# Two transformer blocks with a 32-expert MoE on one core: expert counts read into registers once, one extra path of 32 slots, bias load queued behind a weight tile

## The chip, the core and the metric

The kernel runs on one core of a Trainium2 chip. The metric is device time in microseconds (us) from the first to the last work of one execution. Before the change three runs took 1896.96, 1898.42 and 1899.1 us; their median, 1898.42 us, is the number that the change is measured against. The trace read here is a further execution of the same program, taken by the hardware profiler.

## The reference, cut to what matters

256 tokens of width 1024 pass a first block of two layers (attention, gated linear attention, dense feed-forward) and a second block whose feed-forward part is a mixture of 32 experts. Each token goes to its four best experts, and all arithmetic is in float32. The part that the change touches is the expert stage, with W = `w_gate_up` (32 x 1024 x 2048) and V = `w_down` (32 x 1024 x 1024):

```python
logits = (xt @ w_router) + b_router
top_v, top_i = lax.top_k(logits, 4)
gates = softmax(top_v)
for e in range(32):                       # as the reference's sorted blocks do it
    rows = tokens that chose e            # their number is the expert's count
    hdn = xt[rows] @ W[e] + b_gate_up[e]
    glu, lin = minimum(hdn[:, :1024], 7), clip(hdn[:, 1024:], -7, 7)
    y = (glu * sigmoid(1.702 * glu) * (lin + 1)) @ V[e] + b_down[e]
    out[rows] += gate[rows, e] * y
```

A count can be anything from 0 to 256, so the kernel must be right for all of them. The mean is 32 tokens per expert.

## The kernel before, in words

The program is unrolled: 32 copies of the expert's code follow one another. TensorE (PE) multiplies, VectorE (DVE) and ScalarE (ACT) evacuate and do the activation, GpSimd (POOL) makes small selectors, SyncE (SP) issues the weight loads. A scheduler places the instructions of each engine in an order close to that of the source, and every engine works its own list in that order.

**Weights.** An expert is 12 tiles of 1 MB, eight of W and four of V (`class Expert`, L1158). `etile` (L1149) hands out 18 buffers in the cyclic order of `RING2`, so 1.5 experts fit; the last of the 18 is the memory of `h`. SP issues one DMA for each tile (L1167 for W, L1175 for V), in order, and waits with each until the buffer's former readers are done. Ten tiles of expert 0 are issued while the second block's attention still runs (`EARLY`), the other two just before the expert loop (`first.rest()`).

**The 64 common slots.** `slots` (L1126) gives each token its place among an expert's tokens (`posm`) and writes the 32 counts and their maximum into `cnt`. `spread` (L1112) makes one-hot columns from it in `pos`, and `pick_up` (L1371) multiplies the tokens with them, so that `xt` holds the transposed inputs of two experts at a time: 64 slots of each of the two experts, and 64 further slots of each, 256 columns in all. `g1` (L1206) multiplies the 64 slots with W, `bias` (L1224) adds the bias through a one-hot selector `pick` that POOL writes, `act` (L1230) applies the activation, `g2` (L1242) multiplies with V, and `combine` (L1294) adds the result to the tokens.

**More than 64 tokens.** The count of an expert is needed in a register of PE, ACT and DVE, because each of the three branches on it. `count` (L1395) has POOL copy one number of `cnt` to a 1x1 tile (from expert 2 on behind POOL's last `pick`, by `issue_after`), and each of the three engines loads that number into a register. In the loop, `tc.If(n > 64)` (L1465) holds `extra_in` for slots 64 to 95 and, in a nested `tc.If(n > 96)` (L1467), a second `extra_in` for slots 96 to 127. After `g2` stands a second pair of branches (L1501, L1503) with `extra_out`. An engine whose branch isn't taken jumps over the code of the body. `extra_in` reads W and `extra_out` reads V, so that the buffers of W are given back behind the branch of L1465, those of V behind that of L1501.

**More than 128 tokens.** After the last expert, `many` (L1405) branches on the largest count, and would loop over all experts again, four chunks of 32 slots each.

**The expert biases.** `load_bias` (L1217) loads `b_gate_up` into `ball` on SP's queue, and ACT and DVE split it. It is traced in the loop's first turn, before `expert(1)` is loaded, and `bias(banks, 0)` needs it late in expert 0.

Of the kernel before, what the change touches and what calls it, by code (L numbers as in the profile page):

```python
# [9 lines left out]
F32 = mybir.dt.float32  # L10
BF16 = mybir.dt.bfloat16
F32R = mybir.dt.float32r
I32 = mybir.dt.int32
# [7 lines left out]
P = 128  # L21
T = 256
D = 1024
KC = D // P
DFF = 2816
NF = DFF // P
NE = 32
# [6 lines left out]
HOME = 99  # L34
RING2 = (-1, 0, 1, -1, 2, 3, 4, 5, 6, 7, -1, -1, 8, 9, 10, 11, 12, HOME)
EARLY = 10


C_ROPE = 0
# [56 lines left out]
def kernel_body(ctx, tc, I, out, stop=None, dbg=None):  # L96
    nc = tc.nc
# [10 lines left out]
    order = {}  # L108

    def nm(s):  # L110
        uid[0] += 1
        return f"{s}_{uid[0]}"
# [673 lines left out]
    with ExitStack() as cx:  # L786
# [44 lines left out]
        x = xT()  # L831
# [287 lines left out]
        def first_up(ts=(0, 1), kcs=range(KC)):  # L1119

# [37 lines left out]
        class Expert:  # L1158
# [4 lines left out]
            def load(self, n):  # L1163
                for _ in range(n):
                    r = etile()
                    if len(self.ws) < KC:
                        self.queue.dma_start(r, self.up(len(self.ws)))  # L1167
# [23 lines left out]
    with ExitStack() as cx:  # L1191
# [6 lines left out]
        now = mo.tile([P, 6, NE], F32, name="now", bufs=1)  # L1198
# [17 lines left out]

        def load_bias():  # L1217
            ball = mo.tile([P, 2, 512], F32, tag="yh", name="ball", bufs=1)
            for i in range(2):
                nc.sync.dma_start(ball[64 * i:64 * i + 64], I["b_gate_up"].rearrange("(b r) f -> r b f", b=2))  # L1220
            S.copy(bb, ball)
            V.tensor_sub(bb[64:], ball[64:], bb[64:].bitcast(F32))

# [146 lines left out]

        def pick_up(banks=None):  # L1371

            n = 2 if banks is None else 4
# [7 lines left out]
            x = mo.tile([P, KC, T], F32, tag="xt", name=nm("xt"), bufs=1)  # L1381
            for i, q in enumerate(banks):
                (V.tensor_copy if i % 2 else S.copy)(x[:, n * i:n * i + n, :512 // n], q.rearrange("p (a b) -> p a b", a=n))
            return x

        def begin(e, w):

            banks = [psum.tile([P, 512], F32, tag="g1", name=nm("g1")) for _ in range(2)]
            xe = xt[:, :, 64 * (e % 2):64 * (e % 2) + 64]
            g1(banks, xe, w.ws, range(AHEAD))  # L1390
            if e:
                bias(banks, e)
            return w, banks, xe, xt[:, :, P + 64 * (e % 2):P + 64 * (e % 2) + 64]

        def count(e):  # L1395

            ne = spool.tile([1, 1], I32, tag="ne", name=nm("ne"), bufs=2)
            if e > 1:
                with tc.issue_after(order[G].ins):
                    G.tensor_copy(ne, cnt[0:1, e:e + 1])  # L1400
            else:
                G.tensor_copy(ne, cnt[0:1, e:e + 1])
            return nc.values_load(ne[0:1, 0:1], engines=ARMS, min_val=0, max_val=T)

        def many(spare):  # L1405

            cmax = spool.tile([1, 1], I32, tag="ne", name="cmax", bufs=2)
            V.tensor_copy(cmax, cnt[0:1, NE:NE + 1])
            most = nc.values_load(cmax[0:1, 0:1], min_val=0, max_val=T)
            with tc.If(most > P):  # L1410
                V.tensor_scalar_add(now[:, 0:2, :], posm, -128.0)
                V.tensor_copy(now[:, 2:4, :], gate)
                V.tensor_copy(now[:, 4:6, :], qe)
                a1, pg = spare[:, :256], spare[:, 256:]
                with tc.For_i(0, NE, 1) as ei:
                    w = Expert(lambda kc: I["w_gate_up"][bass.ds(ei, 1), kc * P:(kc + 1) * P, :].rearrange("o p f -> (o p) f"),
                               lambda b: I["w_down_2"][bass.ds(ei, 1), b * 256:(b + 1) * 256, :].rearrange("o p f -> (o p) f"))
                    w.rest()
                    for c in range(4):
                        extra_in(a1, extra_xt(32 * c, lambda t: now[:, t, 0:1]), lambda q: now[:, 4 + q, 0:1], w.ws)  # L1420
                        extra_out(a1, 32 * c, lambda t: now[:, t, 0:1], lambda t: now[:, 2 + t, 0:1], w.wd, pg)
                    then = mo2.tile([P, T], F32, tag="oT", name="then", bufs=1)[:, :6 * NE].rearrange("p (a e) -> p a e", a=6)
                    V.tensor_copy(then[:, :, :NE - 1], now[:, :, 1:])
                    V.tensor_copy(now[:, :, :NE - 1], then[:, :, :NE - 1])
# [10 lines left out]
        n = count(0)  # L1435
        y = last = None
        for e in range(NE):
            j = e % 2
            w, banks, xe, xs = nxt
            if j == 0:  # L1440
                pT, gs = ahead
            if j and e + 1 < NE:
                spread(e + 1)
            if e == 0:
                load_bias()
                g1(banks, xe, w.ws, range(AHEAD, KC - 1))
                bias(banks, 0)
            g1(banks, xe, w.ws, range(KC - 1 if e == 0 else AHEAD, KC))
            through = order[TE].ins
            if e + 1 < NE:  # L1450
                nw = expert(e + 1)
# [10 lines left out]
            more = [mo2.tile([P, 256], F32, tag="og", name=nm("og"), bufs=2) for _ in range(2)]  # L1462
            pm, gt = (lambda t: posm[:, t, e:e + 1]), (lambda t: gate[:, t, e:e + 1])
            sel = lambda q: qe[:, q, e:e + 1]
            with tc.If(n > 64):  # L1465
                extra_in(more[0], xs[:, :, 0:32] if e > 1 else extra_xt(64, pm), sel, w.ws)
                with tc.If(n > 96):  # L1467
                    extra_in(more[1], xs[:, :, 32:64] if e > 1 else extra_xt(96, pm), sel, w.ws)
            if e + 1 == NE:
                gp2 = mo.tile([P, 2 * D], F32, tag="xt", name="gp2", bufs=1)  # L1470
# [6 lines left out]
            if e + 1 < NE:  # L1477
                after = count(e + 1)
            with tc.issue_after(through):
                if j and e + 1 < NE:  # L1480
                    xt = pick_up()
# [17 lines left out]
                    carry(fin)  # L1499
            g2(a, w.wd, y, j)  # L1500
            with tc.If(n > 64):  # L1501
                extra_out(more[0], 64, pm, gt, w.wd)
                with tc.If(n > 96):  # L1503
                    extra_out(more[1], 96, pm, gt, w.wd)
                if e + 1 == NE:
                    carry(fin, True)
            if e + 1 < NE:
                nxt = begin(e + 1, nw)
                n = after
            if j:  # L1510
                last = pT, y
        r = []
# [52 lines left out]
```

## Time and profile before

| what | us |
|---|---|
| runs: lowest, median, highest | 1896.96, 1898.42, 1899.1 |
| the profiled execution's own time | 1897.12 |
| its span, first to last instruction | 1895.3 |
| first matmul of expert 0 in the span (L1212) | 832.09 |
| PE busy in the span | 1715.2 |

The span is what the profile's rows add up to; 1.8 us lie around it, and the execution stands 1.3 us under the median. Some 832 us pass before the first matmul of the expert stage. In the rows below, PE is the matrix multiply, PEld the weight load that runs beside it, and an engine's name with q (PEq, SPq) its instruction sequencer. A float32 matmul leaves two records on PE and two on PEld. "Waited for" lists say what ended the idle time of an engine, with its sum and the number of times.

### The profile page before, as it was taken

What the parts mean: (1) busy time and instruction counts of PE and PEld (TensorE: products, weight loads), DVE (VectorE), ACT (ScalarE), POOL (GpSimd) and SP (SyncE); (2) the same over time, 40 slices, a digit from 0 to 9 for tenths busy, and PEclk for the clock granted to TensorE, in tenths of its full rate; (3) what the DMA queues carried; (4) which work ended last, traced back from release to release, by engine and by line L of the source; (5) the groups of instructions that cost most, each with busy time, mean ns of one, the idle gap of its engine ahead of it and who ended that gap; (6) DMA issues with size and microseconds to landing.
All of it is one profiled execution on the core that took longest, in us unless ns stands there. A gap on an engine that the chain in (4) does not pass through costs nothing. (4 is left out here: it accounts for less than half of the span.)

```text
span 1895.3 us, 23935 instructions
## 1 busy us (share of the span) xinstructions
PE 1715.2 (90%) x9400; PEld 1089.3 (57%) x9400; DVE 801.0 (42%) x1340; ACT 531.1 (28%) x906; POOL 161.6 (9%) x261
## 2 busy tenths in 40 slices
PE   7999999999999999998988888889898888888887
PEld 6887998788799879854333333324433333333332
DVE  5677776667777667542212121213222121212122
ACT  5645444564544446421011010101101110111011
POOL 1131220203122021000000000000000000000000
PEclk9999999999999999979999999999989999999999
DMA  9636788433588865559799999998889999999993
GB/s 307 160 123 203 242 280 298 135 134 123 192 264 273 287 210 181 201 232 372 304 400 409 390 383 412 402 401 339 330 334 414 416 385 397 392 414 401 405 398 117
DMA packets 161023, 571.27 MB, mean 301 GB/s; under 512 B 15490, under 2 KB 66188, under 8 KB 111636
## 3 DMA queue, kind: packets, MB, share of 16 engines
q1 hardware_dynamic: 149848, 553.47, 75.5%
q10 hardware_dynamic: 10140, 12.62, 2.0%
q0 software_dynamic: 800, 1.77, 0.8%
q8 instruction: 181, 2.97, 0.6%
q14 instruction: 54, 0.44, 0.1%
HBM read 564.11 MB, written 3.71 MB: 300 GB/s over the span
## 5 line engine op out<-in xcount | busy, mean ns | idle before, releaser
L1212 PE MATMUL g<-w,xt 128*64 128x512 f32 x2048 | 501.2, 606 | 100.3 <-PEq L1465 46.1
L1212 PEld LDWEIGHTS g<-w,xt 128*64 128x64 f32 x2048 | 157.7, 138 | 417.2 <-issue 411.6
L249 DVE TENSOR_TENSOR wlo<-w,whi 128x1024 fp32r<-128x1024 f32 x203 | 256.3, 1268 | 101.6 <-ACT whi L248 94.0
L248 ACT CAST whi<-w 128x1024 fp32r<-128x1024 f32 x203 | 211.2, 1046 | 176.4 <-PE ps L255 88.4
L1255 PE MATMUL ps<-w,aT 128*64 128x512 f32 x1024 | 230.2, 600 | 22.8 <-ACT aT L1249 22.8
L1233 DVE TENSOR_SCALAR g<-g 128x512 f32<-128x512 f32 x32 | 22.1, 692 | 490.5 <-PE g L1212 490.5
L254 PE MATMUL ps<-xh,whi 128*128 128x256 f32 x792 | 227.4, 287 | 0.0
L256 PE MATMUL ps<-xl,whi 128*128 128x256 f32 x792 | 223.4, 282 | 0.0
L255 PE MATMUL ps<-xh,wlo 128*128 128x256 f32 x792 | 223.3, 282 | 0.0
L1234 ACT ACTIVATE g<-g 128x512 f32<-128x512 f32 x32 | 19.3, 602 | 547.1 <-DVE g L1233 547.1
L1255 PEld LDWEIGHTS ps<-w,aT 128*64 128x64 f32 x1024 | 85.9, 138 | 145.8 <-issue 116.3
L254 PEld LDWEIGHTS ps<-xh,whi 128*128 128x128 f32 x792 | 149.4, 189 | 1.8 <-PE ps L403 1.2
L255 PEld LDWEIGHTS ps<-xh,wlo 128*128 128x128 f32 x792 | 149.2, 188 | 1.8 <-issue 1.4
L256 PEld LDWEIGHTS ps<-xl,whi 128*128 128x128 f32 x792 | 149.3, 188 | 0.0
L1258 DVE TENSOR_TENSOR yl<-ps,yh 64x512 fp32r<-64x512 f32 x64 | 44.1, 688 | 246.7 <-ACT yh L1257 245.7
L1257 ACT CAST yh<-ps 64x512 fp32r<-64x512 f32 x64 | 37.1, 579 | 230.2 <-PE ps L1255 229.4
L1226 POOL CAST pick<-qe 128x128 fp32r<-128x128 f32 x32 | 9.5, 296 | 970.5 <-PE g L1228 969.7
L254 PE MATMUL ps<-whi,xh 128*128 128x512 f32 x176 | 72.5, 412 | 2.0 <-ACT xh L212 1.1
L255 PE MATMUL ps<-whi,xl 128*128 128x512 f32 x176 | 71.0, 404 | 1.5 <-DVE xl L213 1.5
L256 PE MATMUL ps<-wlo,xh 128*128 128x512 f32 x176 | 70.4, 400 | 0.0
L489 DVE SCALAR_TENSOR_TENSOR modm<-w,cond,modm 128x512 f32<-128x512 f32 x84 | 65.4, 779 | 7.8 <-DMA w<-in_w_ada_dram 6.2
L746 POOL TENSOR_TENSOR al<-sg,ah 128x256 fp32r<-128x256 f32 x36 | 44.5, 1237 | 209.4 <-ACT ah L745 209.4
(375 smaller groups left out, 2343.4 us busy)
## 6 DMA issues: line engine op xcount, KB each, us to landing
w<-in_w_gate_up_dram SPq DMA_DIRECT2D x256, 1024.0 KB, 12.1
w<-in_w_down_dram SPq DMA_DIRECT2D x149, 1024.0 KB, 12.7
w<-in_w_in_dram SPq DMA_DIRECT2D x32, 1024.0 KB, 6.2
w<-in_w_ada_dram SPq DMA_DIRECT2D x24, 1024.0 KB, 5.2
w<-in_w_gate_dram SPq DMA_DIRECT2D x22, 1024.0 KB, 8.3
w<-in_w_up_dram SPq DMA_DIRECT2D x22, 1024.0 KB, 5.3
w<-in_w_out_dram SPq DMA_DIRECT2D x12, 1024.0 KB, 4.9
w<-in_w_in_dram SPq DMA_DIRECT2D x8, 512.0 KB, 8.8
```

Of the source, the lines that this page charges most:

```text
L248: S.copy(hv, self.raw)
L249: V.tensor_sub(lv, self.raw, hv.bitcast(F32))
L254: TE.matmul(o, lhsT=ah, rhs=bh, start=first, stop=False)
L255: TE.matmul(o, lhsT=al, rhs=bh, start=False, stop=False)
L256: order[TE] = TE.matmul(o, lhsT=ah, rhs=bl, start=False, stop=last)
L489: V.scalar_tensor_tensor(m, w, c, m, ALU.mult, ALU.add)
L746: G.tensor_tensor(out=al[:, f, :], in0=a, in1=ah[:, f, :].bitcast(F32), op=ALU.subtract)
L1212: order[TE] = TE.matmul(banks[b][64 * a:64 * a + 64, :], lhsT=xt[:, kc, :], rhs=ws[kc][:, c0:c0 + 512], start=kc == 0, stop=kc == KC - 1)
L1233: V.tensor_scalar(out=a, in0=gl, scalar1=7.0, scalar2=None, op0=ALU.min)
L1255: TE.matmul(q[at[b], :], lhsT=aT[:, f % 4, 64 * (f // 4):64 * (f // 4) + 64], rhs=wd[f // 2][:, c0:c0 + 512], start=f == 0, stop=f == KC - 1)
L1257: S.copy(y[0][at[b], b, :], q[at[b], :])
L1258: V.tensor_tensor(out=y[1][at[b], b, :], in0=q[at[b], :], in1=y[0][at[b], b, :].bitcast(F32), op=ALU.subtract)
```

## The change

It has four parts.

1. **Counts.** `count` is gone. Before the loop, one call loads all 32 numbers of `cnt` into registers of PE, ACT and DVE, checked against 0 and 256 as each number was before. POOL copies nothing, and `n = counts[e]` in the loop.
2. **Extra path.** Only slots 64 to 95 remain in the loop: one `extra_in` and one `extra_out` for each expert, no nested branch. `pos` shrinks from 256 to 192 columns, `pick_up` multiplies 192 instead of 256 columns and copies 384 instead of 512 columns of each bank, and the spare tile `og` has one buffer instead of two.
3. **Last branch.** `many` now runs from 97 tokens instead of 129. It loads each expert's count in its loop, skips experts that have no more than 96, and does five chunks from slot 96 on instead of four from slot 128 on.
4. **Bias load.** The first six tiles of expert 1 are issued before `load_bias`, and the two bias loads are ordered on SP behind the 18th tile.

The diff, cut:

```diff
-    pos = cpool.tile([P, 2, 2 * P], F32R, name="pos")
+    pos = cpool.tile([P, 2, 192], F32R, name="pos")
...
-                    for i in range(2 if e else 1):
-                        onehot(pos[:, t, P * i + 64 * j:P * i + 64 * j + 64], 64 * i, posm[:, t, e + j:e + j + 1])
+                    onehot(pos[:, t, 64 * j:64 * j + 64], 0, posm[:, t, e + j:e + j + 1])
+                    if e:
+                        onehot(pos[:, t, P + 32 * j:P + 32 * j + 32], 64, posm[:, t, e + j:e + j + 1])
...
+            with tc.issue_after(held):
+                for i in range(2):
+                    nc.sync.dma_start(ball[64 * i:64 * i + 64], I["b_gate_up"].rearrange("(b r) f -> r b f", b=2))
...
-                            TE.matmul(banks[kc // 2][:, T * (kc % 2):T * (kc % 2) + T], lhsT=part[:, t, kc * P:(kc + 1) * P], rhs=pos[:, t, :],
+                            TE.matmul(banks[kc // 2][:, 192 * (kc % 2):192 * (kc % 2) + 192], lhsT=part[:, t, kc * P:(kc + 1) * P], rhs=pos[:, t, :],
...
-        def count(e):
-
-            ne = spool.tile([1, 1], I32, tag="ne", name=nm("ne"), bufs=2)
-            if e > 1:
-                with tc.issue_after(order[G].ins):
-                    G.tensor_copy(ne, cnt[0:1, e:e + 1])
-            else:
-                G.tensor_copy(ne, cnt[0:1, e:e + 1])
-            return nc.values_load(ne[0:1, 0:1], engines=ARMS, min_val=0, max_val=T)
...
-            with tc.If(most > P):
-                V.tensor_scalar_add(now[:, 0:2, :], posm, -128.0)
+            with tc.If(most > 96):
+                V.tensor_scalar_add(now[:, 0:2, :], posm, -96.0)
...
+        counts = []
+        for i in range(0, NE, NREG):
+            counts += nc.values_load_multi_w_load_instructions(cnt[0:1, i:i + NREG], engines=ARMS, min_val=0, max_val=T)[1]
         xt = pick_up(g["xt"])
...
+            n = counts[e]
...
             if e == 0:
+                nw = expert(1)
+                nw.load(len(RING2) - KC - KC // 2)
+                held = order["load"].ins
                 load_bias()
...
             with tc.If(n > 64):
-                extra_in(more[0], xs[:, :, 0:32] if e > 1 else extra_xt(64, pm), sel, w.ws)
-                with tc.If(n > 96):
-                    extra_in(more[1], xs[:, :, 32:64] if e > 1 else extra_xt(96, pm), sel, w.ws)
+                extra_in(more, xs if e > 1 else extra_xt(64, pm), sel, w.ws)
...
             with tc.If(n > 64):
-                extra_out(more[0], 64, pm, gt, w.wd)
-                with tc.If(n > 96):
-                    extra_out(more[1], 96, pm, gt, w.wd)
+                extra_out(more, 64, pm, gt, w.wd)
```

`NREG` is 32, so the loop around the load runs once.

## Rows read from the trace of the kernel before

**Rows 1.** Windows: us, five engines' busy time, granted PE clock, DMA share, GB/s.

```profile
860.00:880.00 20.00, 19.50 (x214) 10.65 (x210) 2.16 (x5) 1.53 (x3) 0.00 (x0) 1.00 1.01 419
900.00:920.00 20.00, 18.38 (x134) 8.61 (x132) 4.63 (x12) 2.27 (x5) 0.00 (x0) 1.00 0.56 228
...
930.00:1272.00 342.00, 293.29 (x1338) 123.20 (x1340) 76.75 (x155) 36.90 (x74) 4.57 (x22) 0.99 0.98 399
1420.00:1831.00 411.00, 352.80 (x1642) 149.38 (x1640) 90.46 (x186) 46.07 (x94) 5.33 (x25) 1.00 0.99 403
```

**Rows 2.** Line L1212 (`g1`), whole span: PE's idle time, by what ended it, times.

```profile
  PEq L1465: 46.1, 28
  POOL ne L1400: 32.5, 25
  PEq L1501: 8.3, 7
  DMA w<-in_w_gate_up_dram: 6.9, 11
  PEq L1467: 5.2, 1
```

**Rows 3.** Line L1403 on PE's sequencer, whole span, then from 826 to 832 us.

```profile
L1403 PEldq TENSOR_LOAD <-ne x32: 302/308/487, 827.6 to 1795.1; - x32
L1403 PEldq FUSED_REGOPS  x32: 146/152/160, 828.1 to 1795.5; - x32
L1403 PEldq SEQ_ASSERT  x32: 18/18/26, 828.4 to 1795.7; - x32
...
L1403 PEldq TENSOR_LOAD <-ne x2: 312/400/487, 827.6 to 828.4; - x2
```

**Rows 4.** PE in order of time: around the first expert, and the last of `g1`.

```profile
827.48 3.78 PE L1123 MATMUL ps<-pos,xm 128*128 128x128 f32 x16 [0.71 <-DVE pos L1109]
832.09 5.53 PE L1212 MATMUL g<-w,xt 128*64 128x512 f32 x16 [0.83 <-issue]
...
1864.99 1.94 PE L1212 MATMUL g<-w,xt 128*64 128x512 f32 x8 [0.16 <-PEq L1465]
```

**Rows 5.** The branches on PE's sequencer: ns min/median/max; the fourth within 1300 to 1320 us.

```profile
L1465 PEldq COMPARE_BRANCH  x34: 70/6018/6452, 851.2 to 1860.4; - x34
...
L1501 PEldq COMPARE_BRANCH  x32: 70/3302/6760, 863.4 to 1878.7; - x32
...
L1467 PEldq COMPARE_BRANCH  x2: 556/3380/6203, 878.5 to 1315.4; - x2
...
L1467 PEldq COMPARE_BRANCH  x1: 556/556/556, 1315.4 to 1315.4; - x1
...
L1503 PEldq COMPARE_BRANCH  x4: 187/261/348, 915.4 to 1341.5; - x4
```

**Rows 6.** PE's records in the branches' bodies, each by its line.

```profile
L1334 PE MATMUL ps<-w,xt x128: 376/379/403, 1310.2 to 1317.7; 128*32 128x256 f32 x128
...
L1328 PE MATMUL ps<-bb,qe x32: 379/379/403, 872.0 to 1310.0; 128*32 128x256 f32 x32
...
L1319 PE MATMUL ps<-opos,xmh x16: 254/263/263, 868.3 to 871.7; 128*128 128x32 f32 x16
...
L1367 PE MATMUL ps<-w,oaT x128: 378/379/403, 909.0 to 1337.5; 128*32 128x256 f32 x128
...
L1342 PE MATMUL ps<-oaT,oT x32: 374/446/479, 913.1 to 1340.9; 32*128 32x256 f32 x32
```

**Rows 7.** Line L1379 (`pick_up`): half of its matmuls, the other half alike.

```profile
L1379 PE MATMUL ps<-pos,xmh x240: 273/280/582, 893.1 to 1812.5; 128*128 128x256 f32 x120
```

**Rows 8.** SP's queue in order of time, 796 to 858 us.

```profile
796.71 3.66 SPq L1175 DMA_DIRECT2D w<-in_w_down_dram  x3
828.10 1.39 SPq L1220 DMA_DIRECT2D ball<-in_b_gate_up_dram  x2
829.53 27.81 SPq L1167 DMA_DIRECT2D w<-in_w_gate_up_dram  x8
```

More of the change, by code (lines that the diff above doesn't have):

```diff
@@ L36 @@
 EARLY = 10
+NREG = 32
 C_ROPE = 0
@@ L1166, in load @@
                     if len(self.ws) < KC:
-                        self.queue.dma_start(r, self.up(len(self.ws)))
+                        order["load"] = self.queue.dma_start(r, self.up(len(self.ws)))
                         self.ws.append(r)
@@ L1197, in kernel_body @@
         bb = mo.tile([P, 2, 512], F32R, name="bb", bufs=1)
-        now = mo.tile([P, 6, NE], F32, name="now", bufs=1)
+        now = mo.tile([P, 9, NE], F32, name="now", bufs=1)
         qe = mo.tile([P, 2, NE], F32, name="qe", bufs=1)
@@ L1218, in load_bias @@
             ball = mo.tile([P, 2, 512], F32, tag="yh", name="ball", bufs=1)
-            for i in range(2):
-                nc.sync.dma_start(ball[64 * i:64 * i + 64], I["b_gate_up"].rearrange("(b r) f -> r b f", b=2))
+            with tc.issue_after(held):
+                for i in range(2):
+                    nc.sync.dma_start(ball[64 * i:64 * i + 64], I["b_gate_up"].rearrange("(b r) f -> r b f", b=2))
             S.copy(bb, ball)
@@ L1371, in pick_up @@
         def pick_up(banks=None):
-            n = 2 if banks is None else 4
+            n, c = (2, 192) if banks is None else (4, P)
             if banks is None:
@@ L1378, in pick_up @@
                         for i, part in enumerate((xmh, xml)):
-                            TE.matmul(banks[kc // 2][:, T * (kc % 2):T * (kc % 2) + T], lhsT=part[:, t, kc * P:(kc + 1) * P], rhs=pos[:, t, :],
+                            TE.matmul(banks[kc // 2][:, 192 * (kc % 2):192 * (kc % 2) + 192], lhsT=part[:, t, kc * P:(kc + 1) * P], rhs=pos[:, t, :],
                                       start=kc % 2 + t + i == 0, stop=kc % 2 + t + i == 3)
-            x = mo.tile([P, KC, T], F32, tag="xt", name=nm("xt"), bufs=1)
+            x = mo.tile([P, KC, 192], F32, tag="xt", name=nm("xt"), bufs=1)
             for i, q in enumerate(banks):
-                (V.tensor_copy if i % 2 else S.copy)(x[:, n * i:n * i + n, :512 // n], q.rearrange("p (a b) -> p a b", a=n))
+                (V.tensor_copy if i % 2 else S.copy)(x[:, n * i:n * i + n, :c], q[:, :n * c].rearrange("p (a b) -> p a b", a=n))
             return x
@@ L1392, in begin @@
                 bias(banks, e)
-            return w, banks, xe, xt[:, :, P + 64 * (e % 2):P + 64 * (e % 2) + 64]
-        def count(e):
-            ne = spool.tile([1, 1], I32, tag="ne", name=nm("ne"), bufs=2)
-            if e > 1:
-                with tc.issue_after(order[G].ins):
-                    G.tensor_copy(ne, cnt[0:1, e:e + 1])
-            else:
-                G.tensor_copy(ne, cnt[0:1, e:e + 1])
-            return nc.values_load(ne[0:1, 0:1], engines=ARMS, min_val=0, max_val=T)
+            return w, banks, xe, xt[:, :, P + 32 * (e % 2):P + 32 * (e % 2) + 32]
         def many(spare):
@@ L1409, in many @@
             most = nc.values_load(cmax[0:1, 0:1], min_val=0, max_val=T)
-            with tc.If(most > P):
-                V.tensor_scalar_add(now[:, 0:2, :], posm, -128.0)
+            with tc.If(most > 96):
+                V.tensor_scalar_add(now[:, 0:2, :], posm, -96.0)
                 V.tensor_copy(now[:, 2:4, :], gate)
                 V.tensor_copy(now[:, 4:6, :], qe)
+                V.tensor_copy(now[:, 6, :], cnt[:, :NE])
+                V.tensor_scalar_add(now[:, 7:9, :], posm, -224.0)
@@ L1414, in many @@
                 a1, pg = spare[:, :256], spare[:, 256:]
                 with tc.For_i(0, NE, 1) as ei:
[L1416 to L1421, printed above, removed]
@@ L1422, in many @@
-                    then = mo2.tile([P, T], F32, tag="oT", name="then", bufs=1)[:, :6 * NE].rearrange("p (a e) -> p a e", a=6)
-                    V.tensor_copy(then[:, :, :NE - 1], now[:, :, 1:])
-                    V.tensor_copy(now[:, :, :NE - 1], then[:, :, :NE - 1])
+                    one = spool.tile([1, 1], I32, tag="ne", name="one", bufs=2)
+                    V.tensor_copy(one, now[0:1, 6, 0:1])
+                    with tc.If(nc.values_load(one[0:1, 0:1], min_val=0, max_val=T) > 96):
+                        w = Expert(lambda kc: I["w_gate_up"][bass.ds(ei, 1), kc * P:(kc + 1) * P, :].rearrange("o p f -> (o p) f"),
+                                   lambda b: I["w_down_2"][bass.ds(ei, 1), b * 256:(b + 1) * 256, :].rearrange("o p f -> (o p) f"))
+                        w.rest()
+                        for c in range(5):
+                            pm = lambda t: now[:, 7 * (c // 4) + t, 0:1]
+                            extra_in(a1, extra_xt(32 * (c % 4), pm), lambda q: now[:, 4 + q, 0:1], w.ws)
+                            extra_out(a1, 32 * (c % 4), pm, lambda t: now[:, 2 + t, 0:1], w.wd, pg)
@@ L1426, in many @@
+                    for i in range(0, 9, 3):
+                        then = mo2.tile([P, T], F32, tag="oT", name="then", bufs=1)[:, :3 * NE].rearrange("p (a e) -> p a e", a=3)
+                        V.tensor_copy(then[:, :, :NE - 1], now[:, i:i + 3, 1:])
+                        V.tensor_copy(now[:, i:i + 3, :NE - 1], then[:, :, :NE - 1])
             turn[0] -= KC + KC // 2
+        counts = []
+        for i in range(0, NE, NREG):
+            counts += nc.values_load_multi_w_load_instructions(cnt[0:1, i:i + NREG], engines=ARMS, min_val=0, max_val=T)[1]
@@ L1434, in kernel_body @@
             ahead = places(), slot_gates(0)
-        n = count(0)
         y = last = None
@@ L1450, in kernel_body @@
             if e + 1 < NE:
-                nw = expert(e + 1)
+                nw = expert(e + 1) if e else nw
                 nw.rest()
@@ L1461, in kernel_body @@
                 G.memset(acc, 0.0)
-            more = [mo2.tile([P, 256], F32, tag="og", name=nm("og"), bufs=2) for _ in range(2)]
+            more = mo2.tile([P, 256], F32, tag="og", name=nm("og"), bufs=1)
             pm, gt = (lambda t: posm[:, t, e:e + 1]), (lambda t: gate[:, t, e:e + 1])
@@ L1465, in kernel_body @@
             with tc.If(n > 64):
-                extra_in(more[0], xs[:, :, 0:32] if e > 1 else extra_xt(64, pm), sel, w.ws)
-                with tc.If(n > 96):
-                    extra_in(more[1], xs[:, :, 32:64] if e > 1 else extra_xt(96, pm), sel, w.ws)
+                extra_in(more, xs if e > 1 else extra_xt(64, pm), sel, w.ws)
             if e + 1 == NE:
-                gp2 = mo.tile([P, 2 * D], F32, tag="xt", name="gp2", bufs=1)
+                gp2 = mo.tile([P, KC * 192], F32, tag="xt", name="gp2", bufs=1)
                 gp2, spare = gp2[:, :D], gp2[:, D:D + 512]
@@ L1476, in kernel_body @@
                 many(spare)
-            if e + 1 < NE:
-                after = count(e + 1)
             with tc.issue_after(through):
@@ L1508, in kernel_body @@
                 nxt = begin(e + 1, nw)
-                n = after
             if j:
```

## The prediction, made before the changed kernel was run

> **What bounds the kernel now.** I read the windows first [rows 1]. Over the steady stretches of the expert loop (930 to 1272 and 1420 to 1831 us) the DMA engines show a share of 0.98 and 0.99 at 399 and 403 GB/s, and PE is busy 86%. Both look nearly full, so the question is who waits for whom. The window 860 to 880 us, with loads queued throughout, reaches 419 GB/s, so the transfers still have holes of 4 to 5%. The list of what ended PE's idle time before `g1` [rows 2] settles it: 46.1 us went to the branch of L1465 on PE's own sequencer (28 times, 1.65 us each), 32.5 us to POOL's copy of the count (25 times, 1.30 us), 8.3 us to the branch of L1501, and only 6.9 us to weights that hadn't landed. PE sets the pace, and the buffers that it gives back late are the holes in the transfers. The floor behind it is near: a tile is 128 x 2048 float32, 1.049 MB, so an expert's 12 tiles take 12.58 MB / 419 GB/s = 30.0 us, against 12.58 / 0.401 = 31.4 us at the present mean rate.
>
> **The counts.** What goes is POOL's copy behind each `pick` and the three loads behind it: 32.5 us of PE's idle time [rows 2]. The remaining `pick` of POOL has no other customer and stays hidden. What comes is 32 values at once on PE, ACT and DVE, just ahead of expert 0. On PE a value costs a load of 0.308 us and a check of 0.152 us, plus an assertion that takes 0.018 us, 0.48 us in all [rows 3]; 32 of them are 15.3 us. They start about 827.6 us [rows 3] while PE still works through L1123, and expert 0 starts at 832.09 anyway [rows 4], which hides 4.5 us. That leaves **+11 us** in front of expert 0, where everything on PE queues behind it. The bounds: one load for all 32 with 32 checks, 0.31 + 32 x 0.17 = 5.8 us, or +1; and 0.8 us for a value, as the two at 827.6 and 828.4 stand apart [rows 3], 26 us, or +21. I take 0.48 because it is the median of 32 cases. ACT and DVE have no check and are done earlier. [...]
>
> **The branches.** A branch that isn't taken jumps over its body, and on PE that takes very different times [rows 5]. I measure a body in PE records, each with a weight load beside it [rows 6]: `extra_in` has 128 (L1334) + 16 (L1328, 32 in two) = 144, so 288 instructions; `extra_out` has 64 (L1367) + 16 (L1342) and a few transposes, about 168. Today L1465 skips two `extra_in`, 576 instructions, at a median of 6.0 us; L1501 skips 336, at a median of 3.3 us and up to 6.76, and only 7 of its 32 passes cost PE time [rows 2]; the nested L1467 skips 288 at expert 14 and took 0.556 us, while at expert 1, where the body also has 32 matmuls of `extra_xt`, 352 took 6.2 us; the nested L1503 skips 168 and never took over 0.348 us [rows 5]. PE's queue holds matmuls for 6.0 - 1.65 = 4.4 us meanwhile, so that only jumps near 6 us cost PE time. The change makes L1465 a jump of 288 and L1501 one of 168. By the rows, 168 is always short. For 288 there is one case, short; at 336 between a fifth and a quarter are long. I let 1 in 7 stay long, 4 of 28: 4 x 1.65 = 6.6 us stay of the 46.1, **-39.5 us**, and **-8.3 us** at L1501. Bounds: all short, -46; all as now, 0. The nested jump at L1467 goes with its **-5.2 us** [rows 2]. In the two experts that do have more than 64 tokens, no nested body ran, so that no count is over 96: `many` still skips, and its new loop costs nothing.
>
> **The narrower `pick_up`.** 15 calls of 32 matmuls. One takes 0.280 us at 256 columns [rows 7] and 0.263 us at 32 [rows 6], so 64 columns fewer are worth 64/224 x 17 ns = 5 ns: 480 x 5 ns = **-2 us**. The copies of 384 instead of 512 columns on ACT and DVE, and the shorter one-hot writes on DVE, run beside `g2` and cost or give nothing; PE doesn't wait for them now.
>
> **The bias load.** In the queue of SP the last tile of expert 0 is issued by 800.4 us, then the bias load holds the queue until 828.10, and expert 1's first tiles follow from 829.53 [rows 8]. The change lets six tiles, 6 x 2.5 = 15 us of transfer, go into that gap. I cost it at **0**: after those six the 18 buffers are full in either order, and the next can't start before expert 0 gives its W back at its branch, which starts at 851.2 us [rows 5]. PE doesn't wait for these tiles before. If the six come free only after 820 us, the bias lands up to 15 us later than now, about 847 us, which is when expert 0 wants it; with the 11 us of register loads in front it still isn't late.
>
> **The sum.** PE: -32.5 - 39.5 - 8.3 - 5.2 - 2 + 11 = -76.5, a span of 1895.3 - 76.5 = 1819 us. The transfers allow: first release at 851.2 + 11 = 862 us, 366 tiles left x 1.049 MB / 419 GB/s = 916 us, and the hole at expert 1's `extra_out` (228 of 419 GB/s in 900 to 920 us, 9 us [rows 1]) stays: the last tile lands at 1787. The last tile of W lands four tiles, 10 us, ahead of it, at 1777; from the last of `g1` (1864.99) to the end PE needs 1895.3 - 1865.0 = 30.3 us [rows 4]: 1807 us. With two limits this close, each now and then waits for the other. Of today's holes (4.3% of 900 us, 39 us) I let 15 us stay. Span 1819 + 15 = 1834, and with the 1.8 us around the span the execution takes 1836; the profiled execution lies 1.3 us under the median, which I let go into the rounding: **1836 us**.
>
> **Rivals.**
> - *The long jump stays.* L1465 takes 6 us at 288 instructions too. For it: one short case at 288 against one long at 352, and a jump in three staying long would already take 9 us more than I allow. Then PE gains -32.5 - 5.2 - 2 - 8.3 + 11 = -37: 1858, and with some 5 us of transfer waits 1865 us. [...]
> - *The transfers are at their limit already.* The share of 0.98 to 0.99 is the true ceiling and 419 GB/s holds for 20 us only. Then the loop gains 1 to 2% of 930 us, 14 us, and expert 1's nested jump 5, against +11 in front: 1890 us. Against it speak 6.9 us of PE waits for weights in the whole loop.
> - *Slower.* The register loads sit in front of expert 0 at the high price (0.8 us for a value, +21 us), and the transfers are at their limit as above, with the loop gaining its 1% (9 us) and expert 1's jump 5: +21 - 14 = +7, so 1904 us. It decides from +18 on, 0.70 us for a value, and only where the loop can't give time back.
> - *Nothing happens where it counts:* the scheduler leaves the branches behind another late signal of the same length (the next `pick` of POOL in place of the copy), and the gains at the jumps pay for the loads: within 4 us of now.
>
> **How the numbers follow.** The forecast gets 0.60, with 1812 to 1856 as its own range: loads from +1 to +21, jumps from -46 to -33, stayed holes from 0 to 30 us, not all at one end. The long jump gets 0.20 (1855 to 1878), transfers at their limit 0.10, slower 0.05, nothing 0.05. The range of 1810 to 1872 takes in the forecast and most of the long jump. A measurement tells 0.2%, about 4 us, from no change. Faster by more: 0.60 + 0.20 + most of 0.10 and a little of the rest, 0.90; same 0.05; slower 0.05.
>
> **What would show it.** No POOL copy of counts and no PE wait for it; PE's branch of L1465 mostly under 4 us and its wait list near 7 us instead of 46; expert 0 starting near 843 us; the windows of the loop at 410 to 418 GB/s, and PE waiting for weights for tens of us instead of 6.9; six tile issues ahead of the bias load in SP's queue. The prediction is wrong if the jumps stay at 6 us, if the loads take far from 15 us, or if the rate stays at 400 GB/s while PE waits for weights.

## The result, and the profile after

The changed kernel takes 1830.57 us (median of four runs, 1825.96 to 1833.62) where the kernel before took 1897.69 us in the same session: a ratio of 0.9649, with a 95% interval of 0.963 to 0.9668. The profiled execution took 1830.35 us, with a span of 1828.2. Line numbers have moved: the branch behind `g1` is L1472 (L1465 before), the one behind `g2` L1504 (L1501), `g1` itself L1215 (L1212), the register load L1431 and the branch of `many` L1404.

First the windows of the expert loop, columns as in [rows 1]:

```profile
868.50:900.00 31.50, 30.85 (x282) 17.89 (x284) 9.06 (x25) 5.71 (x13) 0.00 (x0) 1.00 0.97 397
900.00:960.00 60.00, 55.26 (x290) 21.20 (x286) 11.49 (x24) 4.63 (x9) 0.59 (x2) 0.97 0.98 403
960.00:1260.00 300.00, 281.76 (x1330) 114.21 (x1328) 74.10 (x162) 36.76 (x78) 2.95 (x10) 0.99 1.01 418
1260.00:1400.00 140.00, 126.52 (x738) 53.18 (x736) 35.07 (x80) 15.29 (x33) 1.71 (x6) 0.95 0.97 401
1400.00:1780.00 380.00, 355.74 (x1635) 139.66 (x1633) 88.64 (x178) 43.77 (x90) 3.84 (x13) 1.00 1.01 418
1780.00:1796.00 16.00, 12.59 (x54) 3.52 (x52) 0.00 (x0) 0.00 (x0) 0.00 (x0) 1.00 0.87 359
```

In the steady stretches (960 to 1260 and 1400 to 1780 us) PE is busy 94% instead of 86%, and the transfers run at 418 GB/s instead of 399 to 403. The holes that PE used to leave in them are gone, except around the two experts with extra tokens (868.5 to 960 us, and 1260 to 1400) and in the last tiles. Next, what PE waited for from 860 to 1830 us (its own waits alone: sum in us, times, longest), the first two lines those of the kernel before and the rest those of the changed one:

```profile
PE g L1212 <- PEq L1465: 44.1, 26, 2.2
PE g L1212 <- POOL ne L1400: 32.5, 25, 1.5
```

```profile
PE ps L1259 <- ACT aT L1253: 22.0, 30, 0.7
PE g L1215 <- PEq L1472: 15.8, 27, 4.2
PE ps L1251 <- DVE g L1244: 8.6, 14, 0.8
PE ps L1346 <- DMA yl<-in_b_down_dram: 4.2, 1, 4.2
PE fin L1312 <- PEq L1404: 4.1, 1, 4.1
PE g L1215 <- SPq L1404: 3.4, 4, 1.9
PE g L1215 <- DMA w<-in_w_gate_up_dram: 2.0, 4, 0.6
```

The wait for POOL's copy is gone. The wait for the first branch fell from 44.1 to 15.8 us, and the second branch no longer appears. The short waits for `aT` were there before (21.3 us) and stayed. The branches themselves, on PE's sequencer (count: shortest/median/longest in ns, first and last start), beside [rows 5], and the register loads beside [rows 3]:

```profile
L1472 PEldq COMPARE_BRANCH  x34: 70/335/6215, 863.2 to 1792.9; - x34
L1472 PEldq EVENT_SEMAPHORE  x30: 51/51/51, 868.5 to 1794.8; - x30
...
L1504 PEldq COMPARE_BRANCH  x34: 70/330/2705, 877.4 to 1811.7; - x34
...
L1431 PEldq FUSED_REGOPS  x32: 146/146/160, 831.6 to 840.5; - x32
L1431 PEldq SEQ_ASSERT  x32: 18/18/24, 831.9 to 840.7; - x32
L1431 PEldq TENSOR_LOAD <-cnt x1: 2333/2333/2333, 829.2 to 829.2; - x1
```

The median jump at the first branch is 0.335 us where it was 6.018. Listed one by one, 5 of the 30 that are jumped (experts 2, 11, 12, 17 and 27) still take about 6 us. All 32 values come with a single load of 2.33 us, but the 32 checks behind it run from 831.6 to 840.7 us, 0.28 us each. The second line is used below: it is the point behind a jumped branch at which PE gives the tiles of W back. Its first time, 868.5 us, is the first release of W, its last belongs to the last expert; before, it ran from 856.5 to 1864.9 us. Last, SP and PE by time, at the start of the loop and at its end (start, us, what, and in brackets the idle time before it), beside [rows 4] and [rows 8]:

```profile
814.78 14.04 SPq L1170 DMA_DIRECT2D w<-in_w_gate_up_dram  x6
828.87 1.39 SPq L1224 DMA_DIRECT2D ball<-in_b_gate_up_dram  x2
868.62 0.82 SPq L1170 DMA_DIRECT2D w<-in_w_gate_up_dram  x2
...
829.12 3.78 PE L1126 MATMUL ps<-pos,xm 128*128 128x128 f32 x16 [0.70 <-DVE pos L1111]
840.86 4.57 PE L1215 MATMUL g<-w,xt 128*64 128x512 f32 x12 [7.96 <-issue]
...
1792.85 1.94 PE L1215 MATMUL g<-w,xt 128*64 128x512 f32 x8 [1.88 <-SPq L1404]
1795.34 1.94 PE L1215 MATMUL g<-w,xt 128*64 128x512 f32 x8 [0.55 <-SPq L1404]
1801.35 6.49 PE L1312 MATMUL fin<-acc,idio 128*128 128x512 f32 x8 [4.08 <-PEq L1404]
```

Six tiles stand ahead of the bias load, and then SP issues nothing until the first release. At the end PE takes the last tiles of W one at a time, 2.49 us apart, which is 1.049 MB / 418 GB/s = 2.51 us: there it follows the transfers.

### The profile page after: what moved, and what is told of

Read it like the earlier page. It is cut to its first block, busy times and chain, and to the rows that moved or that the text cites. A ratio compares the mean times of both kernels' runs of the same rounds, so it can differ in the third digit from the quotient of the medians.

```text
span 1828.2 us, 23744 instructions
## 1 busy us (share of the span) xinstructions
PE 1710.2 (94%) x9400; PEld 1068.3 (58%) x9400; DVE 795.9 (44%) x1340; ACT 528.2 (29%) x906; POOL 157.4 (9%) x229
## 5 line engine op out<-in xcount | busy, mean ns | idle before, releaser
L1215 PE MATMUL g<-w,xt 128*64 128x512 f32 x2048 | 502.6, 604 | 33.9 <-PEq L1472 15.8
L1215 PEld LDWEIGHTS g<-w,xt 128*64 128x64 f32 x2048 | 153.6, 138 | 354.6 <-issue 328.0
L1259 PEld LDWEIGHTS ps<-w,aT 128*64 128x64 f32 x1024 | 71.9, 138 | 157.5 <-issue 126.1
L1262 DVE TENSOR_TENSOR yl<-ps,yh 64x512 fp32r<-64x512 f32 x64 | 44.1, 689 | 251.3 <-ACT yh L1261 250.3
```

The costliest lines, as they stand in the source:

```text
L1215: order[TE] = TE.matmul(banks[b][64 * a:64 * a + 64, :], lhsT=xt[:, kc, :], rhs=ws[kc][:, c0:c0 + 512], start=kc == 0, stop=kc == KC - 1)
L1259: TE.matmul(q[at[b], :], lhsT=aT[:, f % 4, 64 * (f // 4):64 * (f // 4) + 64], rhs=wd[f // 2][:, c0:c0 + 512], start=f == 0, stop=f == KC - 1)
L1262: V.tensor_tensor(out=y[1][at[b], b, :], in0=q[at[b], :], in1=y[0][at[b], b, :].bitcast(F32), op=ALU.subtract)
```

## The experiments

The kernel before ran beside each: its median was 1895.26 us beside the first four told here, 1894.68 beside "the whole body twice" and "fewer bytes", and 1897.68 beside the rest. Since these medians differ by 3 us, a small difference from the changed kernel is also given by the ratios, each to the kernel before that ran beside it. They stand here by what they ask.

**Part 1 alone.** The kernel before with all counts loaded at once:

```diff
-            if e + 1 < NE:
-                after = count(e + 1)
+            n = counts[e]
```

> The kernel before with the first part alone: all counts loaded at once, the nested branch, the 256 columns and the bias load as before. Theory (PE set the pace before, the transfers set it after the whole change): PE loses the 32.5 us of waits for the counts and gains 7 to 11 us of loads in front of expert 0; the jumps at the first branch stay near 6 us with some 40 us of idle time, so PE still sets the pace: 1868 to 1878 us. Rival (the count and the jump are one wait, and without the count the jump hides itself behind a fuller queue): the jumps' idle time falls too, under 1855 us. Rival (the loads cost more than the waits): 1890 us or more.

Measured 1889.28 us, ratio 0.997 (0.9954 to 0.9986): 6 us of gain where 17 to 27 were expected. PE's waits from 860 to 1830 us in this kernel:

```profile
PE g L1214 <- PEq L1470: 48.7, 28, 2.0
...
PE g L1214 <- PEq L1504: 8.8, 9, 1.1
PE ps L1381 <- issue: 8.5, 5, 3.3
...
PE g L1214 <- issue: 3.9, 1, 3.9
```

The 32.5 us of waits for POOL's copy are gone, but the branch costs 4.6 us more than before and the two "issue" waits, which came to 1.9 us before, 12.4. Between the first and the last release the loop took 993.7 us (862.5 to 1856.2) against 1008.4: 14.7 us won. The first release came 6.0 us later, and the stretch behind the last release grew from 30.4 to 34.6 us. That makes -14.7 + 6.0 + 4.2 = -4.5 us, the difference of the two spans (1890.8 and 1895.3). This wait did not take its whole length with it (14.7 of 32.5 us): about half of it covered sequencer time that then showed by itself. These "issue" waits stand behind long jumps (the one of 3.9 us begins at 1122.2 us, 0.8 us after a jump of 6.2 us); what they are, no row names.

**Parts 2 to 4 alone.** The changed kernel with a copy and three loads per expert again:

```diff
-            n = counts[e]
+            if e + 1 < NE:
+                after = count(e + 1)
```

> The changed kernel with its first part undone: POOL copies each count and three engines load it per expert, as before the change; the short jumps, 192 columns and the bias load behind the 18th tile stay. Theory (after the change the transfers set the pace at 418 GB/s): the waits for counts, 1.3 us per expert, come back on PE, but PE's expert then takes about 29.7 us and the transfers' 30.1, so the waits replace waits for weights, and the 7 us of loads in front of expert 0 go: 1822 to 1838 us, within 8 us of the changed kernel. Rival (PE still sets the pace, so that idle times add up): 1830 + 32.5 - 7 = 1855 us.

Measured 1828.09 us (1827.34 to 1828.31), ratio 0.9644 (0.9628 to 0.966): as fast as the whole change, so nearly all of the gain comes from the extra path. PE waits for the copy again, less than before:

```profile
PE g L1215 <- POOL ne L1404: 12.8, 10, 1.3
PE g L1215 <- PEq L1479: 10.6, 26, 1.9
```

It pays 12.8 us there in place of the checks ahead of expert 0, and its first release comes at 858.3 instead of 868.5 us. The first part of the change is worth nothing here.

**The bias load back in front.**

```diff
-                nw = expert(1)
-                nw.load(len(RING2) - KC - KC // 2)
-                held = order["load"].ins
                 load_bias()
+                nw = expert(1)
```

> The changed kernel with its fourth part undone: the bias load is issued ahead of expert 1's tiles and holds the queue until 828 us. Theory (18 buffers are full in either order before expert 0 gives its first tiles back): 0, within 4 us of 1830.6. Rival (15 us of transfers moved ahead of the loop are 15 us won in a loop that the transfers bound): 1840 to 1846 us.

Measured 1826.23 us (1825.77 to 1829.07), 4.3 us under the changed kernel by the medians, but only 1.7 by the ratios (0.964, with 0.9622 to 0.9658, beside 0.9649), whose intervals overlap. The totals alone do not show a difference; the traces show where one would come from. PE's bias matmuls of expert 0, in this kernel and then in the changed one:

```profile
839.30 5.18 PE L1215 MATMUL g<-w,xt 128*64 128x512 f32 x16 [8.01 <-issue]
...
853.85 0.73 PE L1231 MATMUL g<-bb,pick 128*128 128x512 f32 x2
```

```profile
859.09 0.72 PE L1232 MATMUL g<-bb,pick 128*128 128x512 f32 x2
```

From expert 0's first matmul to its bias it is 14.6 us here and 18.2 in the changed kernel. PE doesn't stand still in between: the scheduler, presumably because it takes the bias to come later, puts 16 more matmul records of `g1` ahead of it (72 instead of 56), which can only be expert 1's. So expert 0 ends later, and with it the first release, 863.3 us here against 868.5. Of these 5.2 us, 1.6 were there before expert 0 began: the profiled execution of the changed kernel was that late already at L1126, and three other runs with part 4 (parts 2 to 4 alone, no checks, the whole body twice) were not. The order of the bias is left with 3.6 us.

**No checks on the registers.**

```diff
-engines=ARMS, min_val=0, max_val=T)[1]
+engines=ARMS, min_val=0, max_val=T, skip_runtime_bounds_check_because="...")[1]
```

> The changed kernel without the 32 checks of the counts on PE (each count lies in 0 to 256 anyway); the one load of 2.3 us stays and hides behind the matmuls before it. Theory (expert 0's start sets the first release of buffers, and the transfers stand still until then, so a delay there goes to the end in full): expert 0 starts 7 to 8 us earlier and the kernel ends 7 to 8 us earlier, 1822 to 1824 us. Rival (the loop has slack somewhere that swallows a late start): within 3 us of 1830.6.

Measured 1822.91 us (1821.5 to 1823.9), 7.7 us under the changed kernel by the medians and 5.5 by the ratios (0.962, with 0.9604 to 0.9636, beside 0.9649); the first release comes at 858.2 us, 10.3 earlier. Expert 0's start and the load on PE:

```profile
832.27 3.65 PE L1215 MATMUL g<-w,xt 128*64 128x512 f32 x16 [0.83 <-issue]
...
L1431 PEldq TENSOR_LOAD <-cnt x1: 2327/2327/2327, 852.9 to 852.9; - x1
```

Expert 0 begins 8.6 us earlier: 7.1 of them are the idle time ahead of it, 0.83 instead of 7.96 us, and 1.5 belong to the late L1126 of above. A further 1.7 us lie between its first matmul and the release. There the first 16 matmul records took 5.42 us in the changed kernel, with a granted clock of 0.50 from 840.86 to 844.46 us, and 3.65 us here, with 1.00 from 832.27 to 836 us. In the kernel before, whose idle time ahead of expert 0 was 0.83 us, they took 5.53 us [rows 4], with 0.50 from 832.09 to 835.8 us, so these 1.7 us are not shown to be a price of the checks. The load itself moved in this run, to just ahead of the first branch. That it costs nothing where it stands in the changed kernel shows in that kernel's own rows: it ends at 831.5 us, while the matmuls of L1126 go on to 832.9. So the price of part 1 ahead of the loop is the checks, not the load.

**The whole body twice.** `extra_in` runs twice in the branch, without nesting, so that the jump has the length of before:

```diff
-                extra_in(more, xs if e > 1 else extra_xt(64, pm), sel, w.ws)
+                xo = xs if e > 1 else extra_xt(64, pm)
+                for _ in range(2):
+                    extra_in(more, xo, sel, w.ws)
```

> The changed kernel with the extra input path written twice in a row inside the first branch, without nesting: the jump over it is 576 instructions again, and in the two experts that enter it the second pass repeats the first. Theory (the length of the jump decides): most jumps at the first branch take about 6 us again, PE waits 35 to 45 us for them in all, and since that brings PE's expert to the transfers' 30.1 us, the time rises by 5 to 25 us, to 1836 to 1856 us. Rival (the nested branch, not the length, made the jumps slow): the median stays near 0.34 us and the time within 8 us of 1830.6, for the two second passes.

Measured 1879.82 us (1876.69 to 1886.1), ratio 0.9929 (0.9908 to 0.9951): three quarters of the gain are gone, more than was expected. Some 12 of these 49 us are the second passes (below).

```profile
L1472 PEldq COMPARE_BRANCH  x34: 70/6071/7066, 861.7 to 1842.2; - x34
...
PE g L1215 <- PEq L1472: 41.2, 24, 2.3
...
PE g L1215 <- issue: 6.1, 2, 3.6
PE ps L1383 <- issue: 2.4, 1, 2.4
```

The jumps are long again, and from release to release an expert takes 28.9 and 30.5 us in turn where it took 27.3 and 28.8. The second passes in the two experts that need them come to about 12 us (67.1 against 62.7 us and 82.5 against 74.7). Two single experts took 38.8 and 37.6 us; 3.6 and 2.4 us of "issue" waits fall into them, which the changed kernel lacks but for 0.6 us, and the rest stays open. Neither the second passes at this price nor these two experts were in the expectation.

**Half the body more.** Only the first half of `extra_in` is done twice, for a jump of 452 instructions:

```diff
+                extra_in(more, xo, sel, w.ws, range(KC // 2))
                 extra_in(more, xo, sel, w.ws)
```

> The changed kernel with the first half of extra_in done twice (the first pass is overwritten), so that the branch has to jump 452 instructions where it is not taken, against 292 in the changed kernel and 580 with the whole body twice. Theory (whether a jump is long depends on where it lies in the stream as well as on its length, so that the number of long ones grows with the length: 5 of 28 at 292, 8 of 30 at about 336, all at 580): 14 to 24 of 28 take about 6 us, each costs 1.65 us, and the second pass in two experts some 7 us: 1853 to 1870 us. Rival 1 (one limit of length just above 292, so that all are long): 1874 to 1882. Rival 2 (one limit between 452 and 580): 5 or so stay long, 1835 to 1840.

Measured 1846.54 us (1841.96 to 1851.93); 20 of the 30 jumps took over 4 us, as the theory has it, and the median is

```profile
L1472 PEldq COMPARE_BRANCH  x34: 70/5952/6255, 864.1 to 1812.6; - x34
...
PE g L1215 <- PEq L1472: 37.0, 28, 3.1
```

Neither rival of one fixed limit holds. The time stays under the range expected: 15 more long jumps of 1.65 us and 10 us of second passes (70.1 against 62.7 us, 77.3 against 74.7) make 35 us of PE time, an estimate, and the span grew by 22 (1850.2 against 1828.2; this was the slowest of its four runs, and between the medians it is 16). PE had some 13 to 19 us in hand.

**Fewer bytes.** Two of the eight tiles of W are loaded half (11 MB an expert), in the changed kernel and in the one before:

```diff
-self.queue.dma_start(r, self.up(len(self.ws)))
+c = D if len(self.ws) >= FULL else 2 * D
+self.queue.dma_start(r[:, :c], self.up(len(self.ws))[:, :c])
```

> The changed kernel with the last two of the eight W tiles of each expert loaded by half (its gate columns, which then stand in for the linear ones too): 11 MB for an expert instead of 12, the same number of transfers and of matmuls. Theory (the transfers set the pace of the changed kernel): their floor falls from 30.1 to 27.6 us for an expert, PE's 28.4 to 28.8 us take over, and 25 to 40 us go: 1790 to 1806 us; PE's waits for weights fall to a few us. Rival (PE still sets the pace): within 5 us of 1830.6.

> The kernel before with the same two W tiles of each expert loaded by half (the gate columns stand in for the linear ones). Theory (PE set the pace before, with 6.9 us of waits for weights in all): at most those 6.9 us go, 1889 to 1898 us, and the transfers stand still for a larger share. Rival (the transfers' share of 0.98 was the limit already): 11/12 of the loop's bytes, 40 us or more less, under 1860 us.

Measured 1826.78 us (1825.67 to 1827.7) after and 1892.18 us (1887.17 to 1893.71) before. The second lies in its range, the first is a miss. In the first PE's list of waits has none for weights left, and PE fills the time by itself:

```profile
940.00:1260.00 320.00, 304.08 (x1392) 121.52 (x1390) 75.76 (x164) 37.93 (x80) 3.25 (x11) 1.00 0.98 391
```

But its experts take 28.1 and 29.6 us in turn, 0.8 more than in the changed kernel. The busy time of `g1` shows where they go. From 820 to 1890 us, the first three lines are the kernel before, then with fewer bytes, then with more bytes (the next pair), and the last three the changed kernel in the same order:

```profile
820.00:1890.00 1070.00, 501.17 (x2048) 157.72 (x2048) 0.98 0.91 369
820.00:1890.00 1070.00, 522.34 (x2048) 165.75 (x2048) 0.98 0.86 339
820.00:1890.00 1070.00, 472.31 (x2048) 154.52 (x2048) 0.97 0.93 377
...
820.00:1890.00 1070.00, 502.58 (x2048) 153.59 (x2048) 0.97 0.90 369
820.00:1890.00 1070.00, 519.32 (x2048) 161.40 (x2048) 0.98 0.84 338
820.00:1890.00 1070.00, 495.20 (x2048) 146.45 (x2048) 0.97 0.92 376
```

The same 2048 records keep PE busy for 472 to 522 us; why is not shown. With fewer bytes `g1` was 16.7 us longer in the changed kernel and 21.2 in the one before. So the edit changed PE's time as well as the bytes, in both kernels, and neither run tells the two limits apart. In the kernel before, the 21.2 us cost nothing: the wait at the first branch fell by as much (24.6 against 46.1 us, from 860 to 1880 us), and it is matmuls of `g1` that PE works off during that jump (4.45 us of the 6.45 us from 1017.5 us on in the kernel before). The next pair leaves the matmuls' operands alone.

**More bytes.** One transfer of 0.262 MB per expert that nobody reads, in both kernels:

```diff
                 nw.rest()
+                nc.sync.dma_start(mo.tile([P, 512], F32, tag="dummy", ...), I["w_gate_up"][e, :P, :512])
```

> The changed kernel with one more transfer per expert that nobody reads: 128 x 512 float32, 0.262 MB, issued on SP behind the expert's last tile. At the 418 GB/s of its steady windows this is 0.63 us an expert, 19 us in 30 experts. Theory (PE and the transfers are within a few us of each other over the whole loop, as the sum had it): nearly all of it shows, 1842 to 1852 us, with PE waiting for weights for 15 us or more. Rival 1 (PE alone sets the pace and the transfers only look full, because they refill their lead): under 5 us more, 1830 to 1836. Rival 2 (the transfers alone set the pace all along, not only at the end): the full 19 us and more, 1849 to 1856, with the wait spread evenly over the experts.

> The same extra transfer of 0.262 MB per expert in the kernel before. Theory (PE set the pace there, with transfers at 399 to 403 of 418 GB/s): the holes take up most of it, 1895 to 1901 us. Rival (the transfers were at their limit before too): 19 us more, about 1914.

Measured 1845.59 us (1843.1 to 1848.7) after and 1899.39 us (1895.59 to 1905.45) before, the latter with a ratio of 1.002 (1.0003 to 1.0037). So with the same 19 us of transfers the kernel before took 1.7 us longer (3.8 by the ratio), and the changed one 15.0 (13.9). But the transfers did not come alone: `g1` was 28.9 us shorter in the kernel before and 7.4 in the changed one (lines above), and PE's waits for weights in the kernel before, from 860 to 1880 us, rose from 1.8 to 12.4 us. So the 1.7 us are not the price of the bytes by themselves. That transfers were not the limit before is shown by the change itself: from the first to the last release, nearly the same bytes took 926 instead of 1008 us, with `g1` as long as before. PE's waits in the changed kernel with more bytes, from 940 to 1560 us and from 1560 to 1815 us:

```profile
PE g L1215 <- DMA w<-in_w_gate_up_dram: 6.1, 12, 0.6
...
PE g L1215 <- DMA w<-in_w_gate_up_dram: 14.1, 27, 0.6
```

Up to about 1530 us most of its experts take 26.5 to 27.3 and 28.8 us in turn, PE's own pace (26.5 where `g1` is shorter), although the transfers need 12.84 MB / 418 GB/s = 30.7 us for each. PE lives on tiles that were loaded ahead. These run low, and from 1564.3 us on eight experts take 249.2 us, 31.2 each. The changed kernel does the same more mildly: mostly 27.3 and 28.8 us in turn up to 1614 us, then six experts in 180.7 us, 30.1 each, which is 12.58 MB / 418 GB/s to the tenth.

**The two corrections together**, bias load in front and no checks:

> The changed kernel without the 32 bounds checks on PE and with the bias load back in front of expert 1's tiles. Theory (the two gains, 7.7 us and 4.3 us, come at the same place, the first release of W: one moves it from 868.5 to 858.2 us, the other to 863.3): they add only in part, 1818 to 1823 us. Rival (they are the same microseconds): 1823 or more. Rival (they add in full): about 1818.

Measured 1819.31 us (1818.83 to 1821.52), ratio 0.9592 (0.9571 to 0.9613): 11.3 us under the changed kernel, where the two alone gave 7.7 and 4.3 (10.8 by the ratios, where they gave 5.5 and 1.7), so they add almost in full. It is the fastest of all. Expert 0 and the first release in it:

```profile
832.44 3.65 PE L1215 MATMUL g<-w,xt 128*64 128x512 f32 x16 [0.83 <-issue]
...
L1470 PEldq EVENT_SEMAPHORE  x30: 51/51/51, 855.7 to 1782.7; - x30
```

| kernel | first release | span | from the one to the end |
|---|---|---|---|
| changed kernel | 868.5 | 1828.2 | 959.7 |
| bias load in front | 863.3 | 1824.0 | 960.7 |
| no checks | 858.2 | 1819.2 | 961.0 |
| both | 855.7 | 1816.6 | 960.9 |
| parts 2 to 4 alone | 858.3 | 1826.5 | 968.2 |
| half the body more | 869.4 | 1850.2 | 980.8 |
| more bytes | 869.5 | 1846.5 | 977.0 |
| part 1 alone | 862.5 | 1890.8 | 1028.3 |
| before | 856.5 | 1895.3 | 1038.8 |

Each line is one profiled execution. What stands ahead of the first release was paid nearly one for one (12.8 us earlier, 11.6 us shorter), and behind it the kernel took 960 to 961 us in the first four lines, where neither bytes nor PE's work change.

## Why the prediction was right

The forecast was 1836 us, the measurement 1830.57, inside the forecast's own range. The mechanism that carried it was right, but several terms were not, and errors of both signs met in the sum; that it came within 6 us is luck.

- **Who sets the pace before.** Right: not the transfers. The changed kernel moves nearly the same bytes in a loop 82 us shorter, at 418 instead of 399 to 403 GB/s. But it was PE's jumps and waits that set the pace rather than its matmuls: with fewer bytes, 21.2 us more of `g1` cost nothing, because the wait at the branch fell by as much. The runs with fewer and with more bytes stayed within 4 us of the kernel before, but `g1` changed in both, so they prove less than was expected of them.
- **The shorter jump.** Right, and the main gain. The reading of [rows 5] that 288 instructions are mostly short, with 4 of 28 left long, met 5 of 30, though it rested on one case at 288 and a count at 336. Putting the length back cost 49 us, some 12 of them for the second passes. The wait lists of [rows 2] promised -47.8 for the two branches; they fell from 46.1 + 8.3 to 15.8, so by 38.6. What was sized wrong is the remainder, put at 6.6 us: 27 waits are left, the longest of 4.2 us. The nested jump went as said. The rival in which the long jump stays falls.
- **The counts, -32.5.** This step failed. It took a list of waits for time that can be had. Alone, the part shortened the loop by 14.7 us; beside the shorter jumps the copy costs 12.8 us of waits in all; and net of the price in front, the part is worth nothing or costs some 2 us.
- **Register loads, +11.** Expert 0 began 8.8 us later (840.86 against 832.09), 1.6 of them because L1126 began later; the idle time itself is 7.1 us longer. Without the checks the time fell by 7.7 us (5.5 by the ratios). The term was near, but made of the wrong parts: not 32 loads but one, and a check costs 0.28 us, not 0.15 to 0.17. ACT and DVE were not done earlier: their loads stand at 861.6 and 864.2 us, and no wait of PE for them shows. The one load took 2.33 us for 32 values, which is 73 ns for each.
- **The bias load, 0.** This step failed by 3.6 us in the traces (4.3 between the medians, 1.7 by the ratios). It asked when the bias would land, but not where PE's list would then have it: the scheduler moved the bias matmul, and with it the end of expert 0.
- **The sum.** PE's limit was put at 1819, that of the transfers at 1807, and 15 us added because they are close. Close they are, but in the other order (the estimate for PE is below). The chain of transfers is too short by 21 us in three places. The first release was taken as the branch's start (851.2 + 11 = 862) instead of the release behind it (856.5, and 868.5 in fact): 6.5 us. From there to the last tile of `g1` at 1795.3 it took 926.8 us instead of 1777 - 862 = 915: 11.8 us. The windows above add up to 382.8 MB in 927.5 us, 11.7 us more than at a steady 418 GB/s, where the sum had allowed a hole of 9 us, and the 382.8 MB are 3.2 MB more than the sum's 362 tiles (smaller loads, and tiles of V already under way), 7.7 us. From that tile to the end it took 32.9 us instead of 30.3, with 4.08 us at the branch of `many` where it had been 2.60 us. 1807 + 6.5 + 11.8 + 2.6 = 1828, the span. PE alone would have ended 5 to 19 us earlier, an estimate between the waits for tiles in its list (3.4 + 2.0 us) and the 13 to 19 us in hand with half the body more. So the 15 us that brought the sum to 1834 had a reason that does not hold: they stood for mutual waiting, and the time went into a chain that started late and had holes.
- **The rival of transfers at their limit already** falls for the kernel before, since 418 GB/s holds for 380 us on end. It comes near to the kernel after. The rival that is slower falls with it.
- **The signs.** Expert 0 near 843 us (840.86), windows at 410 to 418 GB/s (418), six tiles ahead of the bias and no POOL copy came as named. The wait at the first branch near 7 us came as 15.8, and the tens of us of waiting for weights did not come: PE lives on its lead for 750 us and waits only behind 1614 us.
- **The narrower `pick_up`**, -2 us, was not tried by itself and stays open.

## What to carry to other kernels

A branch that is mostly skipped was paid here by the length of its body (a median of 6.018 us at 576 instructions, 0.335 us at 292), so keep rare code out of the hot loop and move it behind one branch at the end. Sum a list of waits only after asking what each of them covers; of 32 us of waits removed, 15 were won. And once transfers run full (418 GB/s here), look at what stands ahead of the first release of a buffer: there every microsecond counted nearly one for one here, be it a bounds check on a register or a load's place in a queue.

## What the runs showed of the hardware

- **The time of a skipped branch on PE went by the length of its body, and at one length it differed from expert to expert.** Of the passes that jump, over 4 us took: none of 30 at about 168 instructions (2.7 us at most), 5 of 30 at 292, 8 of 30 at about 336 (L1501 in the kernel before), 20 of 30 at 452, 27 of 30 at 576 (L1465 in the kernel before) and 27 of 30 at 580. Below 4 us lie not only short ones: at 336, ten more took 2.7 to 3.8 us. The long ones at 292 were experts 2, 11, 12, 17 and 27 in the changed kernel, and the same five with the bias load in front and with more bytes; with fewer bytes it was expert 22 in place of 2. Without the checks, where PE's code ahead of the loop is shorter, they were experts 5, 6, 15, 21 and 26, and these five again, with expert 25, with the two corrections together. That the place in the code decides is the author's estimate from these sets. Which experts jump long is not explained by any run.
- **A long jump of 6 us cost 1.65 us of PE's time** (46.1 us in 28 waits), as PE worked off what was queued meanwhile (4.45 us of the 6.45 us of the jump at 1017.5 us), and 0.95 us where `g1` was 21.2 us longer in all (24.6 us in 26 waits); but some came with a further stop of 2.4 to 3.9 us marked "issue".
- **The same matmuls did not always take the same time.** 2048 records of `g1` kept PE busy for 472 to 522 us in the six kernels listed under "fewer bytes"; the cause is open.
- **The DMA engines held 418 GB/s for 380 us** with PE busy 94% beside them. The share of the windows then reads 1.01, so that the 0.98 of before was no ceiling.
